# Second feed-forward re-ordered so that down pieces alternate with block pieces; rope scores with 128 rows

## The chip, the core and the metric

The kernel runs on one core of one Trainium2 chip. Its time is the device time of the whole program in microseconds (us), the median of three runs: 2722.33 us before the change (2721.0 to 2722.39). Five engines work side by side and meet at semaphores: TensorE (PE, matmuls; its weight loads are shown apart as PEld), VectorE (DVE), ScalarE (ACT), GpSimd (POOL) and SyncE (SP, which here starts all weight transfers).

## The reference

Two transformer blocks run one after the other on 256 tokens of width 2048, in float32. Cut to what the change touches:

```python
# first block: attention with 16 heads; a head has 128 plain and 64 rotated (rope) dimensions
q = concat([q[..., :128], apply_rope(q[..., 128:], positions)])
k = concat([k[..., :128], apply_rope(k[..., 128:], positions)])
s = einsum('bqhd,bkhd->bhqk', q, k) * scale        # causal softmax, then times v
x = x + (silu(h2 @ w_ffn_gate) * (h2 @ w_ffn_up)) @ w_ffn_down     # width 5632
# second block: stick-breaking attention, spatial gating, then
h2 = rms_norm(x, g_ff)
x = x + square(relu(h2 @ w_ff1)) @ w_ff2            # w_ff1 2048 x 8192, w_ff2 8192 x 2048
```

## The kernel before

Every weight matrix is cut into **pieces** of two 128-row tiles by 512 columns (512 KB). SP brings a piece into a raw buffer (tile R, or tile G for block pieces). ACT rounds it to a shorter float (line 230, "high part", into tile W), DVE subtracts that from the raw numbers (line 232, "low part"), and PE multiplies. A product of two floats is made of three matmuls: high by high, high by low, low by high. The activations stand transposed and split the same way in A, B or C.

There are two kinds of piece. A **plain** piece (`chunk`, lines 262 to 264) is 2 row tiles x 2 token tiles x 3 = 12 matmuls with 512 columns. A **block** piece (`strassen`, lines 315 to 317) treats the same product as a 2 x 2 block product with seven products in place of eight: 7 x 3 = 21 matmuls with 256 columns. It needs three more DVE operations ahead (`sums`, lines 207 to 209, which make the sums of weight blocks) and longer casts (1792 in place of 1024 columns), and at the end of its chunk `fin` (lines 328 to 332) adds the seven products up from PSUM banks 0 to 3. A chunk is the 8 pieces that make 512 output columns of a 2048-row matrix.

All work is a list `jobs`, which `drive` (line 161) emits in order. Before the matmuls of piece k it emits the split (DMA, sums, cast, low part) of the pieces up to k + 3, where a slot of W is free: plain pieces of the feed-forwards rotate over three slots, block pieces over two. Each engine executes its own instructions strictly in the order of emission and waits at semaphores. `run` entries of the list (transposes, evictions) stand between pieces.

In the first feed-forward `braid` mixes a plain chunk (gate) with a block chunk (up) in the order p p s p s p s p s p s p s p s s, where p is plain and s is block. In the second, groups of two such braids (an ff1 chunk that is plain, the next that is block) are followed by the down product `w_ff2` in plain pieces: 4 chunks of 8 pieces for each of the four groups. So 8 of its 16 ff1 chunks are block chunks. A down chunk collects in banks (4, 5), (0, 1), (4, 5), (2, 3) and is added to the residual X on DVE (`ev_acc`, line 907, or `ev_out`, line 1206, which also writes the output). `t_a` transposes 512 columns of activations into B (8 PE transposes, 2 casts, 2 low parts). At the start of each feed-forward `transposed_s` makes the last quarter of its input with sums of blocks (lines 361 to 379).

In the attention `s_pair` makes the scores of two heads, eight groups of three matmuls: four for the 128 plain dimensions, and four for the 64 rope dimensions, whose operands lie on partitions 0 to 63 for one head and 64 to 127 for the other (`hp`).

Of the kernel before, what the change touches and what calls it, by code (L numbers as in the profile page):

```python
# [15 lines left out]
P = 128  # L16
# [8 lines left out]
RAWS = 3  # L25
QW = 256
PLAIN, MIX, STR = 0, 1, 2
AHEAD = {PLAIN: 4, MIX: 3, STR: 3}
# [43 lines left out]
def body(tc, d, out):  # L72
# [4 lines left out]
    with tc.manual_schedule(), \  # L77
# [80 lines left out]
        SLOTS = {PLAIN: range(6), MIX: range(3), STR: range(6, 8)}  # L158

        def drive():  # L160
# [3 lines left out]
            seen_h, seen_r, cnt = {}, {}, {}  # L164
            for i, j in enumerate(pcs):
                kind = j[5]

                def cells(s):
                    a, b, w = hslots(s)
                    return [(o + x) // 256 for o in (a, b) for x in range(0, w, 256)]  # L170

                last, s = min((max(seen_h.get(x, -1) for x in cells(s)), s) for s in SLOTS[kind])
                num.append(s)
                free_h.append(last)
                seen_h.update((x, i) for x in cells(s))
                rk = kind == STR
                m = cnt.get(("r", rk), 0)
                cnt[("r", rk)] = m + 1
                slot = (rk, m % (RAWS if rk else RAW))
                rnum.append(slot[1])  # L180
                free_r.append(seen_r.get(slot, -1))
                seen_r[slot] = i
            raws, hl, used = {}, {}, [-1]
            nd, nt, ns = [0], [0], [0]

            def dma():
                while nd[0] < len(pcs) and free_r[nd[0]] < ns[0] and nd[0] < ns[0] + 2 * RAW:
                    i = nd[0]
                    if i in before_dma:
                        before_dma[i]()  # L190
                    src = pcs[i][1]
                    a, n = src.shape[1], src.shape[2]
                    if pcs[i][5] == STR:
                        t = G[:, 2048 + 2048 * rnum[i] : 4096 + 2048 * rnum[i]]
                    else:
                        t = R[:, 1024 * rnum[i] : 1024 * rnum[i] + 1024]
                    sync.dma_start(t[:, : a * n].rearrange("p (a b) -> p a b", a=a), src)
                    raws[i] = t
                    nd[0] += 1

            def sums(upto):

                while nt[0] <= min(upto, nd[0] - 1):
                    i = nt[0]
                    if pcs[i][5] == STR:
                        v = raws[i].rearrange("p (a b) -> p a b", a=8)
                        dve.tensor_tensor(v[:, 4:6, :], v[:, 0:4:3, :], v[:, 1::-1, :], op=ALU.subtract)  # L207
                        dve.tensor_tensor(v[:, 6, :], v[:, 3, :], v[:, 4, :], op=ALU.subtract)  # L208
                        dve.tensor_tensor(v[:, 7, :], v[:, 2, :], v[:, 6, :], op=ALU.subtract)
                    nt[0] += 1  # L210

            def split(upto):
                while ns[0] <= min(upto, len(pcs) - 1) and free_h[ns[0]] <= used[0]:
# [9 lines left out]
                    if kind == STR:  # L223
                        n, a = 1792, 7
                        t = t[:, 256:]
# [16 lines left out]
            for j in jobs:  # L242
                if j[0] == "run":
                    j[1]()
                else:
                    split(k + AHEAD[j[5]])
                    assert ns[0] > k
                    j[2](*hl.pop(k))
                    used[0] = k
                    k += 1  # L250

# [44 lines left out]
        def strassen(pair, forms, w, kts, c0, evict, later=False):  # L296
# [3 lines left out]
            prod = [(("x", 0, 0), 0, 2, 1), (("x", 1, 0), 1, 0, 0), (("s", 3), 2, 3, 0), (("x", 1, 1), 6, 2, 0),  # L300
                    (("s", 0), 3, 1, 1), (("s", 1), 5, 0, 1), (("s", 2), 4, 1, 0)]

            def mk(j):
                def fn(h, l):
                    opened = set()
                    for x, wi, bank, half in prod:
                        o = PS[:, bank * 512 + half * QW : bank * 512 + (half + 1) * QW]
                        if x[0] == "x":
                            xh, xl = pair(2 * j + x[1], x[2])
                        else:  # L310
                            xh, xl = forms[:, 0, j, x[1], :], forms[:, 1, j, x[1], :]
                        first = j == 0 and bank not in opened
                        opened.add(bank)
                        last = j == kts // 2 - 1
                        pe.matmul(o, xh, h[:, wi, :], start=first, stop=False, skip_group_check=True)  # L315
                        pe.matmul(o, xl, h[:, wi, :], start=False, stop=False, skip_group_check=True)  # L316
                        pe.matmul(o, xh, l[:, wi, :], start=False, stop=last, skip_group_check=True)  # L317
                return fn

            for j in range(kts // 2):  # L320
                items.append(piece(wsrc(w, 2 * j, c0, 512), mk(j), kind=STR))

            def fin():
                q = PS[:, 0:2048].rearrange("p (a b) -> p a b", a=8)
                u = rview(G, 1024, 4, QW)
# [3 lines left out]
                dve.tensor_tensor(u[:, 0:2, :], v[:, 0:1, :].to_broadcast(bc), q[:, 0:2, :], op=ALU.add)  # L329
                dve.tensor_tensor(u[:, 2:4, :], u[:, 1:2, :].to_broadcast(bc), q[:, 2:4, :], op=ALU.add)  # L330
                dve.tensor_tensor(v[:, ::-1, :], u[:, 2:3, :].to_broadcast(bc), q[:, 3:5, :], op=ALU.add)
                dve.tensor_tensor(u[:, 3, :], u[:, 3, :], q[:, 6, :], op=ALU.add)
# [3 lines left out]
            def ends():  # L336
                evict(0, rview(G, 1024, 4, QW)[:, 0:4:3, :])
# [5 lines left out]
        def braid(a, b, inject=None):  # L343

            pa, pb = [x for x in a if x[0] == "pc"], [x for x in b if x[0] == "pc"]
            order = [pa[0], pa[1]]
            for i in range(6):
                order += [pb[i], pa[i + 2]]
            order += [a[-1], pb[6], pb[7], b[-1]]
            for at in sorted(inject or {}, reverse=True):  # L350
                order.insert(at, ("run", inject[at]))
            return order

        def transposed_s(nat, pair, forms, kts, gain):

            x4, s4 = rview(G, 0, 2, 2, NT, P), rview(G, 1024, 2, 4, P)
# [14 lines left out]
            split2(pair.v[:, 0, kts[0] : kts[0] + 4, :], pair.v[:, 1, kts[0] : kts[0] + 4, :], rview(G, 0, 4, S))  # L371
# [304 lines left out]
        qkT = rview(B, 4096, 2, 6, S)  # L676
        pT = [rview(B, 4096 + 3072, 2, 512), rview(C, 2048, 2, 512)]
# [5 lines left out]
        def zero_pT():  # L683
            for t in pT:
                pool.memset(t[:, :, 0:P].bitcast(F32), 0.0)

# [34 lines left out]
        def t_pair(p):  # L721
# [12 lines left out]
            split2(qkT[:, 0, 4:6, :], qkT[:, 1, 4:6, :], bank.rearrange("p (a b) -> p a b", a=2))  # L734

        def s_pair(p):
            rq = rqs[p % 2]
            banks = []
            for h in range(2):
                bank = aux_tile()  # L740
                banks.append(bank)
                for qt in range(NT):
# [3 lines left out]
                    hp = slice(64 * h, 64 * h + 64)  # L746
                    mm3(o, [qkT[hp, i, 4, qs] for i in range(2)], [qkT[hp, i, 5, :] for i in range(2)], False, True)
# [143 lines left out]
        abuf = rview(G, 0, NT, 512)  # L891
# [22 lines left out]
        for gi, (c0, nch) in enumerate(groups):  # L914
            aT = pairat(B, 0, 16)
            for j in range(nch):
                c = c0 + j
                jobs.extend(braid(chunk(h2T, "w_ffn_gate", KT, c * 512, 512, ev_silu, kind=MIX, fixed=(4, 5)),
# [279 lines left out]
        def half(tok, i):  # L1198

            v = rview(G, 1024, 4, QW)[:, 0:4:3, :] if tok == 0 else tmp.rearrange("p (a b) -> p a b", a=2)  # L1200
# [10 lines left out]
        pending = {4: pending}  # L1211
        for gi in range(4):
            aT = pairat(B, 0, 16)
            for j in range(0, 4, 2):
                c = 4 * gi + j
                plain = chunk(h2T, "w_ff1_2", KT, c * 512, 512, lambda tok, ps: relu2(abuf[:, tok, :], tok, ps),
                              kind=MIX, fixed=(4, 5))
                block, ends = strassen(h2T, h2F, "w_ff1_2", KT, (c + 1) * 512, lambda tok, v: relu2(v, tok, v), later=True)
                jobs.extend(braid(plain, block, pending))
                pending = {1: t_a(aT, blocks(abuf), j), 2: ends, 7: t_a(aT, half, j + 1)}  # L1220
            for oc in range(4):
                inj = None
                if oc == 0:
                    inj = {1: pending[2], 2: pending[1], 4: pending[7]}
                    pending = None
                ev = ev_out(oc) if gi == 3 else ev_acc(oc)
                jobs.extend(chunk(aT, "w_ff2_2", 16, oc * 512, 512, ev, row0=16 * gi, inject=inj,
                                  kind=MIX, fixed=DOWN[oc]))


# [17 lines left out]
def blockwise(name, c):  # L1248

    return name == "w_ffn_up" or (name == "w_ff1_2" and c % 2 == 1)  # L1250
# [62 lines left out]
```

## Time and profile before

| | |
|---|---|
| median of three runs | 2722.33 us |
| the profiled execution's own time | 2722.61 us |
| its span, first to last instruction | 2720.9 us |
| PE busy | 2709.6 us (100%) |
| PEld busy | 2278.4 us (84%) |
| DVE busy | 1851.8 us (68%) |
| ACT busy | 1402.6 us (52%) |
| DMA | 506.66 MB, mean 186 GB/s |

The busy time of an engine is the part of the span in which at least one of its instructions was under way. Matmuls are pipelined, so that one that begins every 234 ns may show 400 ns. How fast PE really goes is read from the distances between the starts of its matmuls. The span is 1.7 us shorter than the execution's time.

### The profile page before, as it was taken

The page shows a single profiled execution, that of the slowest core. Times are in us where ns is not written, and L with a number is a line of the kernel's source. Part 1 is how long each engine was busy: PE and PEld are TensorE (multiplying, and loading weights), DVE is VectorE, ACT ScalarE, POOL GpSimd, SP SyncE. Part 2 cuts the span into 40 slices and gives each one's busy share as a digit, 9 for nine tenths or more (in the row PEclk, how much of TensorE's full clock was granted, in tenths as well). Part 3 has the DMA queues.
Part 4 walks back from the last instruction along what each step waited for, and adds up shares of the span by engine and source line. Part 5 has one row for each costly group of instructions (what it writes and reads, how often), then busy time and mean ns, then how long its engine had stood idle before and what let it go on. Part 6 is the DMA issues. An engine that isn't in the chain of part 4 may idle for free. (4 is left out here: it accounts for less than half of the span.)

```text
span 2720.9 us, 35965 instructions
## 1 busy us (share of the span) xinstructions
PE 2709.6 (100%) x13996; PEld 2278.4 (84%) x13996; DVE 1851.8 (68%) x2233; ACT 1402.6 (52%) x1749; POOL 73.0 (3%) x153
## 2 busy tenths in 40 slices
PE   9999999999999999999999999999999999999999
PEld 8988888888888888888888888888888888898887
DVE  6555667766996699579755565455678486685774
ACT  6544666545654455345455555544556355464553
POOL 1000111000000000000000010000000000000000
PEclk9999999999999999999999999999999999999999
DMA  7666534554555555565555554555555555655555
GB/s 255 212 212 201 168 127 146 177 180 172 200 187 179 202 206 186 180 210 185 177 196 172 192 183 166 188 188 181 173 180 182 190 200 177 208 179 185 209 176 164
DMA packets 143179, 506.66 MB, mean 186 GB/s; under 512 B 16160, under 2 KB 18592, under 8 KB 142496
## 3 DMA queue, kind: packets, MB, share of 16 engines
q1 hardware_dynamic: 142864, 504.31, 54.8%
q8 instruction: 109, 1.79, 0.3%
q14 instruction: 62, 0.51, 0.1%
q10 hardware_dynamic: 144, 0.05, 0.0%
HBM read 502.21 MB, written 2.10 MB: 185 GB/s over the span
## 5 line engine op out<-in xcount | busy, mean ns | idle before, releaser
L232 DVE TENSOR_TENSOR W<-R,W 128x1024 fp32r<-128x1024 f32 (+2 forms) x795 | 943.5, 1208 | 508.8 <-ACT W L230 505.4
L230 ACT CAST W<-R 128x1024 fp32r<-128x1024 f32 (+2 forms) x798 | 810.7, 1035 | 532.1 <-PE PS L264 445.1
L263 PE MATMUL PS<-W,A 128*128 128x512 f32 (+2 forms) x1728 | 677.8, 392 | 3.2 <-DVE W L232 3.1
L262 PE MATMUL PS<-W,A 128*128 128x512 f32 (+2 forms) x1728 | 678.5, 393 | 0.6 <-ACT W L230 0.4
L264 PE MATMUL PS<-W,A 128*128 128x512 f32 (+2 forms) x1728 | 675.8, 391 | 0.0
L262 PE MATMUL PS<-W,B 128*128 128x512 f32 (+1 forms) x1248 | 492.0, 394 | 0.0
L263 PE MATMUL PS<-W,B 128*128 128x512 f32 (+1 forms) x1248 | 489.4, 392 | 0.9 <-DVE W L232 0.9
L264 PE MATMUL PS<-W,B 128*128 128x512 f32 (+1 forms) x1248 | 489.3, 392 | 0.0
L230 ACT CAST W<-G 128x1792 fp32r<-128x1792 f32 x152 | 257.5, 1694 | 304.7 <-PE PS L316 173.6
L264 PEld LDWEIGHTS PS<-W,A 128*128 128x128 f32 x1728 | 323.9, 187 | 73.7
L263 PEld LDWEIGHTS PS<-W,A 128*128 128x128 f32 x1728 | 324.4, 188 | 72.5 <-DVE W L232 6.6
L262 PEld LDWEIGHTS PS<-W,A 128*128 128x128 f32 x1728 | 324.2, 188 | 68.3 <-ACT W L230 0.8
L232 DVE TENSOR_TENSOR W<-G,W 128x1792 fp32r<-128x1792 f32 x152 | 307.0, 2020 | 40.6 <-ACT W L230 40.6
L263 PEld LDWEIGHTS PS<-W,B 128*128 128x128 f32 x1248 | 234.1, 188 | 54.6 <-DVE W L232 1.8
L264 PEld LDWEIGHTS PS<-W,B 128*128 128x128 f32 x1248 | 233.9, 187 | 54.2
L262 PEld LDWEIGHTS PS<-W,B 128*128 128x128 f32 x1248 | 234.0, 188 | 53.7
L317 PE MATMUL PS<-W,C 128*128 128x256 f32 x608 | 169.8, 279 | 0.0
L315 PE MATMUL PS<-W,C 128*128 128x256 f32 x608 | 169.8, 279 | 0.0
L316 PE MATMUL PS<-W,C 128*128 128x256 f32 x608 | 169.4, 279 | 0.0
L315 PE MATMUL PS<-W,A 128*128 128x256 f32 x456 | 128.6, 282 | 0.0
L317 PE MATMUL PS<-W,A 128*128 128x256 f32 x456 | 127.3, 279 | 0.8 <-DVE W L232 0.8
L316 PE MATMUL PS<-W,A 128*128 128x256 f32 x456 | 127.3, 279 | 0.0
(231 smaller groups left out, 2481.5 us busy)
## 6 DMA issues: line engine op xcount, KB each, us to landing
R<-in_w_in_dram SPq DMA_DIRECT2D x224, 512.0 KB, 4.5
R<-in_w_ff_dram SPq DMA_DIRECT2D x192, 512.0 KB, 3.6
R<-in_w_ffn_gate_dram SPq DMA_DIRECT2D x88, 512.0 KB, 4.4
G<-in_w_ffn_up_dram SPq DMA_DIRECT2D x88, 512.0 KB, 3.5
R<-in_w_ffn_down_dram SPq DMA_DIRECT2D x88, 512.0 KB, 3.5
R<-in_w_out_dram SPq DMA_DIRECT2D x64, 512.0 KB, 4.3
G<-in_w_ff_dram SPq DMA_DIRECT2D x64, 512.0 KB, 3.5
R<-in_w_attn_o_dram SPq DMA_DIRECT2D x32, 512.0 KB, 4.2
```

What stands on the lines that cost most here:

```text
L230: act.copy(hv, v)
L232: dve.tensor_tensor(lv, v, hv.bitcast(F32), op=ALU.subtract)
L262: pe.matmul(o, x[0], w[0], start=first, stop=False)
L263: pe.matmul(o, x[0], w[1], start=False, stop=False)
L264: pe.matmul(o, x[1], w[0], start=False, stop=last)
L315: pe.matmul(o, xh, h[:, wi, :], start=first, stop=False, skip_group_check=True)
L316: pe.matmul(o, xl, h[:, wi, :], start=False, stop=False, skip_group_check=True)
L317: pe.matmul(o, xh, l[:, wi, :], start=False, stop=last, skip_group_check=True)
```

## The change

There are three parts.

1. **Second feed-forward.** All ff1 chunks from number 2 on are block chunks (14 of 16, `blockwise`), and their pieces alternate with the pieces of the down product of earlier chunks: p s p s ... over 16 pieces (`merge`, `HALF`). In the chunks 3 to 15 the fifth piece is computed in the plain way, but into the same seven-product banks (`flat_fn`, 24 matmuls with 256 columns, kind MIX). The down product is taken in 8 groups of 4 pieces per output chunk (before: 4 groups of 8), so twice as many `ev_acc` are made, and they all collect in banks (4, 5) until the tail. Chunk 0 stands alone as a plain chunk; the gate and up pieces of the first feed-forward go through `merge` too, in the order p s p s.
2. **Block pieces.** The seven products are sorted by bank (0, 1, 2, 3; in the last piece of a chunk 2, 0, 1, 3). The last sum of weight blocks overwrites the first raw block, so a raw buffer is 1792 columns in place of 2048, and chunks from 4 on use four of them (STR4). `mate` stays empty, so `sums` works on one piece at a time as before.
3. **Rope scores.** The keys' rope part of each head gets a slot of its own with 128 rows, of which the other head's 64 are zero (set once by POOL), so that the rope matmuls use all 128 rows. The split of rope queries and keys is 3 casts and 3 low parts in place of one of each. The buffer `pT[0]` moves from B to C.

```diff
-        def braid(a, b, inject=None):
-            pa, pb = [x for x in a if x[0] == "pc"], [x for x in b if x[0] == "pc"]
-            order = [pa[0], pa[1]]
-            for i in range(6):
-                order += [pb[i], pa[i + 2]]
-            order += [a[-1], pb[6], pb[7], b[-1]]
...
+        def merge(pattern, a, b, inject=None):
+            lists, order, n = {"p": list(a), "s": list(b)}, [], 0
+            for c in pattern:
+                if inject and n in inject:
+                    order.append(("run", inject[n]))
+                src = lists[c]
+                order.append(src.pop(0))
+                n += 1
+                while src and src[0][0] == "run":
+                    order.append(src.pop(0))
...
+        BRAID, HALF = "psp" + "sp" * 6 + "s", "ps" * 8
...
+                if kind == STR4:
+                    r = 4 + len(blocks_at) % 4
+                    blocks_at.append(i)
+                else:
+                    r = min((seen_r.get(x, -1), x) for x in (range(5, 8) if kind == STR else range(RAW)))[1]
...
-                        dve.tensor_tensor(v[:, 7, :], v[:, 2, :], v[:, 6, :], op=ALU.subtract)
+                        dve.tensor_tensor(v[:, :, 0, :], v[:, :, 2, :], v[:, :, 6, :], op=ALU.subtract)
...
+                    order = (2, 0, 1, 3) if j == kts // 2 - 1 else (0, 1, 2, 3)
+                    for x, wi, bank, half in sorted(prod, key=lambda t: order.index(t[2])):
...
+                def flat_fn(h, l):
+                    h, l = (t.rearrange("p a (b c) -> p (a b) c", b=2) for t in (h, l))
+                    for kt, tok, wi, bank, half in flat:
+                        three(at(bank, half), pair(2 * j + kt, tok), h[:, wi, :], l[:, wi, :], False, ...)
+                return flat_fn if j in plain else fn
...
-                dve.tensor_tensor(u[:, 3, :], u[:, 3, :], q[:, 6, :], op=ALU.add)
+                if plain:
+                    ends_at = (U[:, 3:4, :], v[:, 1:2, :])
+                    for o, x in zip(ends_at, (q[:, 6:7, :], q[:, 7:8, :])):
+                        dve.tensor_tensor(o, o, x, op=ALU.add)
...
-            split2(qkT[:, 0, 4:6, :], qkT[:, 1, 4:6, :], bank.rearrange("p (a b) -> p a b", a=2))
+            split2(qkT[:, 0, 4, :], qkT[:, 1, 4, :], bank[:, 0:S])
+            for h in range(2):
+                hp = slice(64 * h, 64 * h + 64)
+                split2(qkT[hp, 0, 5 + h, :], qkT[hp, 1, 5 + h, :], bank[hp, S:])
...
-                    hp = slice(64 * h, 64 * h + 64)
-                    mm3(o, [qkT[hp, i, 4, qs] for i in range(2)], [qkT[hp, i, 5, :] for i in range(2)], False, True)
+                    mm3(o, [qkT[:, i, 4, qs] for i in range(2)], [qkT[:, i, 5 + h, :] for i in range(2)], False, True)
...
+        jobs.extend(at_pieces(ff1(0), {3: pending}))
+        block, ends = ff1_blocks(2)
+        jobs.extend(merge(BRAID, ff1(1), block, {3: t_c(0, blocks(abuf))}))
+        pending = {1: t_c(1, blocks(abuf)), 2: ends, 7: t_c(2, half)}
+        for c in range(3, 16):
+            g, o = (c - 3) // 2, 2 * ((c - 3) % 2)
+            block, ends = ff1_blocks(c, (4,), STR4 if c > 3 else STR)
+            jobs.extend(merge(HALF, down(g, o, (4, 5)) + down(g, o + 1, (4, 5)), block, pending))
+            pending = {2: ends, 7: t_c(c, half)}
+        tail = down(6, 2, (4, 5)) + down(6, 3, (0, 1))
+        for oc in range(4):
+            tail += down(7, oc, [(2, 3), (4, 5), (0, 1), (2, 3)][oc])
+        jobs.extend(at_pieces(tail, {2: ends, 5: t_c(15, half)}))
```

How the order of instructions moves is shown for DVE at two places. The first is the start of the first feed-forward, from the end of the last `transposed_s` on. Before:

```order
L379 TENSOR_TENSOR A<-G,A 128x1024
L379 TENSOR_TENSOR C<-G,C 128x1024
L232 TENSOR_TENSOR W<-R,W 128x1024
L207 TENSOR_TENSOR G<-G 128x512
L208 TENSOR_TENSOR G<-G 128x256
L209 TENSOR_TENSOR G<-G 128x256
L232 TENSOR_TENSOR W<-G,W 128x1792
```

And now (line 242 is the old 232, 218 to 220 are the old 207 to 209, 417 is the old 379):

```order
L417 TENSOR_TENSOR A<-G,A 128x1024
L417 TENSOR_TENSOR C<-G,C 128x1024
L218 TENSOR_TENSOR G<-G 128x512
L219 TENSOR_TENSOR G<-G 128x256
L220 TENSOR_TENSOR G<-G 128x256
L242 TENSOR_TENSOR W<-G,W 128x1792
```

The piece that PE needs next after the transposes' cover is used up, the eighth of the braid, was a plain one and is a block one now, and the sums of the block piece after it stand ahead of its low part.

The second place is the end of an ff1 block chunk in the second feed-forward. Before, a braid of two ff1 chunks (line 329 is the first addition of `fin`):

```order
L207 TENSOR_TENSOR G<-G 128x512
L208 TENSOR_TENSOR G<-G 128x256
L209 TENSOR_TENSOR G<-G 128x256
L232 TENSOR_TENSOR W<-G,W 128x1792
L329 TENSOR_TENSOR G<-tmp,PS 128x512
L330 TENSOR_TENSOR G<-G,PS 128x512
L331 TENSOR_TENSOR tmp<-G,PS 128x2x256
L332 TENSOR_TENSOR G<-G,PS 128x256
L232 TENSOR_TENSOR W<-R,W 128x1024
```

And now, a chunk from number 4 on (line 951 is `ev_acc`, the old 907; 354 to 360 are `fin`):

```order
L242 TENSOR_TENSOR W<-G,W 128x1792
L951 TENSOR_TENSOR X<-X,PS 128x512 x2
L242 TENSOR_TENSOR W<-R,W 128x1024
L354 TENSOR_TENSOR G<-tmp,PS 128x512
L355 TENSOR_TENSOR G<-G,PS 128x512
L356 TENSOR_TENSOR tmp<-G,PS 128x2x256
L360 TENSOR_TENSOR G<-G,PS 128x256
L360 TENSOR_TENSOR tmp<-tmp,PS 128x256
L218 TENSOR_TENSOR G<-G 128x512
L219 TENSOR_TENSOR G<-G 128x256
L220 TENSOR_TENSOR G<-G 128x256
L242 TENSOR_TENSOR W<-G,W 128x1792
```

The two evictions of a down chunk stand behind the low part of the next chunk's first block piece, and `fin` has one addition more, 256 columns for the eighth PSUM half that only the plain piece of the chunk uses.

## Rows read from the trace of the kernel before

**Rows 1.** The page, busy us (share of the span) and instructions of each engine.

```profile
PE 2709.6 (100%) x13996; PEld 2278.4 (84%) x13996; DVE 1851.8 (68%) x2233; ACT 1402.6 (52%) x1749; POOL 73.0 (3%) x153
```

**Rows 2.** Waits of PE over the span: total us, times, longest us.

```profile
PE PS L263 <- DVE W L232: 4.1, 6, 0.9
```

**Rows 3.** Timeline of PE: start us, us, engine, line; a plain, then a block piece.

```profile
684.33 0.40 PE L262 MATMUL PS<-W,A 128*128 128x512 f32 x1
...
685.73 0.39 PE L262 MATMUL PS<-W,A 128*128 128x512 f32 x1
...
687.79 0.28 PE L315 MATMUL PS<-W,C 128*128 128x256 f32 x1
...
688.84 0.28 PE L315 MATMUL PS<-W,C 128*128 128x256 f32 x1
```

**Rows 4.** Timeline of PE, the scores of one pair of heads.

```profile
338.62 0.28 PE L262 MATMUL PS<-B 128*128 128x256 f32 x1
...
339.07 0.39 PE L262 MATMUL PS<-B 64*128 64x256 f32 x1
...
342.90 0.50 PE L262 MATMUL PS<-W,B 128*128 128x512 f32 x1
...
343.70 0.40 PE L262 MATMUL PS<-W,B 128*128 128x512 f32 x1
```

**Rows 5.** Groups of PE, 290 to 620 us: count | busy us, mean ns | idle.

```profile
L262 PE MATMUL PS<-B 64*128 64x256 f32 x32 | 12.2, 383 | 0.0
```

**Rows 6.** Groups of DVE by form, 1995 to 2720 us (the second feed-forward).

```profile
L232 DVE TENSOR_TENSOR W<-R,W 128x1024 fp32r<-128x1024 f32 x194 | 236.5, 1223 | 169.8 <-ACT W L230 169.1
L232 DVE TENSOR_TENSOR W<-G,W 128x1792 fp32r<-128x1792 f32 x64 | 129.3, 2020 | 21.3 <-ACT W L230 21.3
L207 DVE TENSOR_TENSOR G<-G 128x512 f32<-128x512 f32 x64 | 43.8, 684 | 2.0 <-DMA G<-in_w_ff_dram 2.0
...
L208 DVE TENSOR_TENSOR G<-G 128x256 f32<-128x256 f32 x64 | 27.2, 425 | 2.2
...
L907 DVE TENSOR_TENSOR X<-X,PS 128x512 f32<-128x512 f32 x24 | 15.3, 681 | 0.0
...
L332 DVE TENSOR_TENSOR G<-G,PS 128x256 f32<-128x256 f32 x8 | 3.3, 414 | 0.0
```

**Rows 7.** Groups of ACT by form, 756.44 to 799.65 us (one braid, first feed-forward).

```profile
L230 ACT CAST W<-G 128x1792 fp32r<-128x1792 f32 x8 | 13.5, 1693 | 19.6 <-DVE G L209 9.9 <-PE PS L316 8.1 <-PE PS L317 1.6
```

**Rows 8.** The same braid: us, busy of PE, PEld, DVE, ACT, POOL, PEclk, DMA, GB/s.

```profile
756.44:799.65 43.21, 43.21 (x274) 38.36 (x272) 41.20 (x49) 23.61 (x21) 0.00 (x0) 1.00 0.56 196
```

**Rows 9.** Timeline of DVE at the braid's beginning: the evictions of the chunk before.

```profile
754.41 0.68 DVE L329 TENSOR_TENSOR G<-tmp,PS 128x512 f32<-128x512 f32 x1
...
757.64 0.74 DVE L899 SCALAR_TENSOR_TENSOR G<-tmp,st,G 128x512 f32<-128x512 f32 x1
```

**Rows 10.** Timeline of PE at the same place.

```profile
756.43 0.39 PE L264 MATMUL PS<-W,A 128*128 128x512 f32 x1
756.75 0.36 PE L315 MATMUL PS<-W,A 128*128 128x256 f32 x1
```

**Rows 11.** Timeline of DVE, start of the first feed-forward, from the low part shown above.

```profile
682.49 1.22 DVE L232 TENSOR_TENSOR W<-R,W 128x1024 fp32r<-128x1024 f32 x1
683.62 0.69 DVE L207 TENSOR_TENSOR G<-G 128x512 f32<-128x512 f32 x1
```

**Rows 12.** Timeline of PE at the same place; in brackets the wait.

```profile
682.70 0.39 PE L262 MATMUL PS<-W,A 128*128 128x512 f32 x1
683.76 0.50 PE L263 MATMUL PS<-W,A 128*128 128x512 f32 x1 [0.68 <-DVE W L232]
...
687.22 0.39 PE L317 MATMUL PS<-W,A 128*128 128x256 f32 x1 [0.39 <-DVE W L232]
```

**Rows 13.** Timeline of PE, start of the second feed-forward.

```profile
2025.66 0.50 PE L263 MATMUL PS<-W,A 128*128 128x512 f32 x1 [0.92 <-DVE W L232]
...
2029.12 0.39 PE L317 MATMUL PS<-W,A 128*128 128x256 f32 x1 [0.40 <-DVE W L232]
```

More of the change, by code (lines that the diff above doesn't have):

```diff
@@ L305, in fn @@
                     opened = set()
[L306 to L312, printed above, removed]
-                        opened.add(bank)
[L314 to L318, printed above, removed]
+                    order = (2, 0, 1, 3) if j == kts // 2 - 1 else (0, 1, 2, 3)
+                    for x, wi, bank, half in sorted(prod, key=lambda t: order.index(t[2])):
+                        xs = pair(2 * j + x[1], x[2]) if x[0] == "x" else [forms[:, i, j, x[1], :] for i in range(2)]
+                        three(at(bank, half), xs, h[:, wi, :], l[:, wi, :], j == 0 and bank not in opened,
+                              j == kts // 2 - 1)
+                        opened.add(bank)
+                def flat_fn(h, l):
+                    h, l = (t.rearrange("p a (b c) -> p (a b) c", b=2) for t in (h, l))
+                    for kt, tok, wi, bank, half in flat:
+                        three(at(bank, half), pair(2 * j + kt, tok), h[:, wi, :], l[:, wi, :], False,
+                              (bank, half) == (3, 1) and kt == 1 and j == max(plain))
+                return flat_fn if j in plain else fn
+            assert 0 not in plain and kts // 2 - 1 not in plain
             for j in range(kts // 2):
-                items.append(piece(wsrc(w, 2 * j, c0, 512), mk(j), kind=STR))
+                items.append(piece(wsrc(w, 2 * j, c0, 512), mk(j), kind=MIX if j in plain else kind))
             def fin():
                 q = PS[:, 0:2048].rearrange("p (a b) -> p a b", a=8)
-                u = rview(G, 1024, 4, QW)
                 v = tmp.rearrange("p (a b) -> p a b", a=2)
@@ L1210, in body @@
         stage(MIX)
[L1211 to L1228, printed above, removed]
+        aT = pairat(B, 0, 16)
@@ new lines, in ff1, with ff1_blocks, down @@
+        def ff1(c):
+            return chunk(h2T, "w_ff1_2", KT, c * 512, 512, lambda tok, ps: relu2(abuf[:, tok, :], tok, ps),
+                         kind=MIX, fixed=(4, 5))
+        def ff1_blocks(c, plain=(), kind=STR):
+            return strassen(h2T, h2F, "w_ff1_2", KT, c * 512, lambda tok, v: relu2(v, tok, v), later=True, plain=plain, kind=kind)
+        def down(g, oc, fixed):
+            at = 8 * (g % 2)
+            return chunk(Pair(aT.v[:, :, at : at + 8, :]), "w_ff2_2", 8, oc * 512, 512, (ev_out if g == 7 else ev_acc)(oc),
+                         row0=8 * g, kind=MIX, fixed=fixed)
```

97 lines of the change are left out of this document (59 added, 38 removed).

## The prediction

> **What bounds the kernel.** I read the page first: PE is busy for 2709.6 of 2720.9 us [rows 1]. Then the waits of PE: the largest entry of the whole program is 4.1 us in six waits for DVE's low part [rows 2]. So PE works without a break, and only two things change the time: the length of its own work, and new waits. Busy time can't give the length, since matmuls overlap in the records; the distance of starts can. In the timeline the reader is to see six plain matmuls begin in 685.73 - 684.33 = 1.40 us, 0.234 us each, and nine block matmuls in 688.84 - 687.79 = 1.05 us, 0.117 us each [rows 3]. A plain piece is then 12 x 0.234 = 2.81 us and a block piece 21 x 0.117 = 2.46 us. The third view is the stretch of one braid: in 43.21 us DVE is busy for 41.20, the granted clock is 1.00 (2.4 GHz), and DMA moves 196 GB/s at a share of 0.56 [rows 8]. DVE is therefore the engine that new waits would come from. ACT with 23.61 us is not.
>
> **Block pieces in the second feed-forward.** Before, 8 chunks x 8 = 64 pieces are block pieces; after, 8 of chunk 2 and 7 of each of the chunks 3 to 15, 8 + 13 x 7 = 99. Thirty-five plain pieces become block pieces, and each saves 12 x 0.234 - 21 x 0.117 = 0.351 us: -12.3 us. The fifth piece of the chunks 3 to 15 is 24 matmuls x 0.117 = 2.81 us, as much as a plain piece. The down product keeps its 128 pieces, and the transposes their number. All of this lies on PE, which sets the end, so it counts in full as long as the pieces are ready in time.
>
> **Are they ready?** A chunk from 4 on has the 16 pieces of the braid of rows 8, with one block piece made plain. On DVE that takes away a low part of 2.02 and the sums 0.684 + 2 x 0.425, in all 3.55 us, and two operations of line 899 (0.74 each [rows 9]), 1.48; it adds a plain low part, 1.22, one addition in `fin`, 0.41, and four evictions of 0.68, 2.72 [rows 6]. 41.20 - 3.55 - 1.48 + 1.22 + 0.41 + 2.72 = 40.5 us. PE takes 43.21 + 0.35 = 43.6 us. DVE's share falls from 95% to 93%, so it has about 3 us in each chunk to make up for a delay.
>
> The tight place is a chunk's end, since each of its two down products collects in banks 4 and 5, and the next one's first matmul must wait until the two evictions have read them. Let the last block piece run from -2.46 to 0. The last down piece ended at -2.46, and the one before began it at -5.27, when the W slot of the next block piece comes free. ACT casts it until about -3.5 (1.69 [rows 7]), DVE's low part follows until -1.5 and stands ahead of the evictions, which end at -0.85 and -0.2. PE wants bank 4 at 0 and bank 5 at 0.70: 0.85 us to spare. Then come a plain low part (to 1.0) and `fin`, five operations of 0.68 and 0.41, to 1.7, 2.3, 2.9, 3.3 and 3.7. The next block piece begins at 2.81, with bank 0 (read by 1.7), then bank 1 at 3.51 (2.9), bank 2 at 4.2 and bank 3 at 4.9 (3.7). The new order of banks has the block piece write first what `fin` reads first. In the middle of a chunk a block piece and eight transposes, over 3 us, cover the evictions. I charge 0.1 us for each of 13 chunk ends, +1.3, for restarts. Bounds: 0, and 13 x 0.7 = 9 if DVE comes 1.55 us later than this.
>
> The Trainium skill (VectorE: DVE Perf Modes, Terms) says that DVE flushes its pipeline after every operation and that the next can't issue until it is empty. The trace shows a low part of 1.22 us begun at 682.49 and the next operation at 683.62, 1.13 us later [rows 11]: they overlap by some 0.1 us. If durations simply added, DVE's share would come closer to PE's time (a rival, below).
>
> **Rope scores.** One pair of heads makes 24 matmuls with 256 columns. They take 342.90 - 338.62 = 4.28 us [rows 4], against 24 x 0.117 = 2.81 by rows 3. The 64-row groups are where PE loses time: there are 32 of these groups [rows 5], and around each the engine leaves the 128-row form and returns to it. The plain matmuls behind the last one need 0.80 us for the first three instead of 0.70 [rows 4], 0.10 more. With 128 rows throughout, the whole excess goes: 8 pairs x (4.28 - 2.81 + 0.10) = -12.6 us. Nothing waits there: no wait on B stands among PE's. The split grows from one cast and one low part of 512 columns to three of 256: about 3 x 0.42 - 0.68 = +0.6 us on DVE and as much on ACT, beside the 4.2 us of two q pieces (24 x 0.175, an estimate at three quarters of rows 3 for 384 columns). I take it as hidden; without that cover it costs 8 x 0.6 = 5 us. The two POOL memsets come once, behind work long done.
>
> **Start of the second feed-forward.** The two waits of 0.92 and 0.40 us [rows 13] come from DVE, which has the last `transposed_s` and the first block pieces to do at once. Now chunk 0 is plain, and the block pieces begin eight pieces later. Each such wait costs about 0.15 us more than its bracket (683.76 - 682.70 - 0.234 = 0.83 for 0.68 [rows 12]): -1.6 us. I bound it at 0 (the waits come back at the first block piece) and -1.8 (both go with all their restarts).
>
> **Start of the first feed-forward.** Its waits of 0.68 and 0.39 us cost 1.4 us with their restarts. In the new order the eighth piece is a block piece. DVE is free for it at 682.49 [rows 11], makes the next sums first (0.684 + 2 x 0.425 = 1.53, to 684.0) and its low part (2.02, to 686.0). PE comes to it at 682.70 as before (a block piece fewer behind the transposes, one more ahead) and wants the low part with its third matmul, at 682.93: 3.1 us of wait in place of 1.4, +1.7. Bounds 0 and +2.5.
>
> **Chunk ends of the first feed-forward.** A braid of 43.21 us has 8 x 2.81 + 8 x 2.46 = 42.1 us of pieces; the remaining 1.1 us is eight transposes and small waits such as the one at 756.75, where the start comes 0.32 us after the last [rows 10] because `fin`, at 754.41 [rows 9], stands behind two block pieces in a row. These are apart now, but the next block piece comes one plain piece sooner. I take -1.0 us over eleven braids; bounds -2.4 and +3.3 (0.3 us more at each).
>
> **Sum.** -12.3 + 1.3 - 12.6 - 1.6 + 1.7 - 1.0 = -24.5 us. From the profiled 2722.6 us this is 2698.1; that execution stands 0.3 us above the median, so 2697.8 us.
>
> **Rivals.**
> *DVE comes late in every chunk.* For it: 93% with waits in between, and 0.85 us of slack. Against: the braids with 95% run with almost no wait. With 0.3 to 0.9 us more at each of 13 ends: 2702 to 2710.
> *The bank pair (4, 5) decides, slower.* The evictions stand behind a low part that DVE only begins when its backlog is done. If DVE ends each chunk a whole block piece (3.55 us) behind, PE waits 3.55 - 0.85 = 2.7 at each end, 35 us in all: 2733. It is slower than before from a backlog of 2.8 us on. The rule of the skill above leads here: added up, 7 x 3.55 + 9 x 1.22 + 2.86 for `fin` + 2.72 + 1.37 for the transposes' low parts is 42.8 of 43.6 us, and a backlog would never be made up. Rows 8 and 11 speak against it: the braid's operations would add up to 8 x 3.55 + 8 x 1.22 + 2.45 + 1.48 + 1.37 = 43.5 us, and are busy for 41.20.
> *The rope groups gain nothing.* If what separates them were a wait and not the change of form, 2710. For it: nothing is seen to release them; against: all groups have the same excess.
> The Trainium skill (TensorE: Matmul & The Clock Gate, Part 3: Packing small matmuls) says that matmuls on different halves of the rows run side by side, so that 128 zero-padded rows would give up a pairing. Rows 4 show no pairing: the eight groups need more time than 24 matmuls one behind the other. By that rule 48 of the 96 rope matmuls are added, 48 x 0.117 = 5.6 us, in place of the gain: 2716.
> *All goes better.* No waits at all: 2692 and below.
>
> **Chances.** Forecast (2693 to 2702) 0.65; DVE late 0.15; bank pair, slower 0.03; rope without gain 0.06, with the lost pairing 0.01; better 0.10. What a measurement can tell from no change is 0.2%, 5.4 us. Only the slower rival and a part of the late one end beyond 2717: faster 0.95, same 0.02, slower 0.03. The range 2691.5 to 2706 leaves out the rope rivals, the slower one and half of the late one.
>
> **What would show it.** In the second feed-forward PE's plain and block starts stay 0.234 and 0.117 apart, a chunk takes 43.6 us, and DVE is busy for about 40 us of it. Waits of line 274 (the old 262) for line 951 would show the bank pair; waits of 276 or of the third block matmul for the low part, a late DVE. The scores of a pair take 2.8 us. In the first feed-forward one wait of some 3 us stands where there were two. If the second feed-forward's chunks take over 45.5 us, the prediction is wrong.

## The result and the profile after

The changed kernel takes 2704.0 us (median; 2702.8 to 2704.7) against 2722.2 us: ratio 0.9934, 95% interval 0.9916 to 0.9951. The profiled span went from 2720.9 to 2702.8 us. The forecast was 2697.8 us in a range of 2691.5 to 2706: the sign and the range hold, and the time is 6.2 us later than forecast. The experiments find 6 to 7 us in the rope part; the misses of the other terms nearly cancel. In number the result lies where the forecast had priced a rival, DVE late in every chunk (2702 to 2710), and that did not happen.

The page of the changed kernel, answering to [rows 1]: PE still works through the whole span, in 471 more and shorter matmuls, and DVE does 116 us more.

```profile
PE 2687.9 (99%) x14467; PEld 2291.7 (85%) x14467; DVE 1968.2 (73%) x2423; ACT 1430.8 (53%) x1771; POOL 74.5 (3%) x155
```

The waits of PE in the changed kernel (total us, times, longest us), answering to [rows 2]. The second, fourth and seventh are new: the transposes of the probabilities waiting for the softmax, a down piece waiting for an eviction, and rope scores waiting for their split.

```profile
PE PS L275 <- DVE W L242: 2.6, 5, 0.8
PE PS L816 <- DVE X L810: 2.1, 2, 1.9
PE PS L324 <- DVE W L242: 1.4, 2, 1.2
PE PS L274 <- DVE X L951: 1.2, 1, 1.2
...
PE PS L274 <- ACT B L416: 0.5, 2, 0.2
```

To see what all this is worth I took, for each matmul of PE, the distance to the next start less the one that its form keeps when nothing disturbs it (0.234 us for 512 columns, 0.175 for 384, 0.117 for 256), and summed this excess by stretch. The cells are good to about 0.4 us. Columns three to five are runs of the experiments below.

| excess, us | before | changed | casts first | raw order | no plain |
|---|---|---|---|---|---|
| up to 300 us | 2.9 | 2.8 | 2.9 | 3.2 | 2.7 |
| attention | 14.3 | 8.6 | 2.2 | 2.2 | 2.2 |
| start of 1st FF, and the 30 us before | 2.5 | 2.5 | 3.0 | 2.6 | 3.3 |
| rest of 1st FF | 3.7 | 2.2 | 2.2 | 2.2 | 2.1 |
| between | 2.4 | 2.4 | 2.4 | 2.4 | 2.4 |
| start of 2nd FF | 1.9 | 1.8 | 1.8 | 1.8 | 1.8 |
| its first chunks | 0.3 | 2.0 | 2.0 | 0.3 | 1.1 |
| its rest | 1.1 | 1.1 | 1.1 | 1.1 | 1.1 |
| sum | 28.9 | 23.2 | 17.4 | 15.5 | 16.6 |

From before to changed the excess falls by 5.7 us. The spans differ by 18.1; the other 12.4 us are the 35 shorter pieces (35 x 0.351 = 12.3).

Two chunks of the second feed-forward (windows; columns as in [rows 8]): PE has no gap, DVE is busy for 40.55 us, as worked out (40.5). A chunk takes 43.22, not 43.6 us.

```profile
2147.10:2190.30 43.20, 43.20 (x277) 38.78 (x276) 40.55 (x49) 24.43 (x24) 0.00 (x0) 1.00 0.55 195
2190.32:2233.54 43.22, 43.22 (x277) 38.80 (x276) 40.55 (x49) 24.43 (x24) 0.00 (x0) 1.00 0.57 196
```

The scores of a pair, timeline of PE, answering to [rows 4]: from the first of 24 matmuls to the plain matmul behind them 2.87 us, and that one's successor comes after 0.24.

```profile
337.27 0.28 PE L274 MATMUL PS<-B 128*128 128x256 f32 x1
...
340.14 0.40 PE L274 MATMUL PS<-W,B 128*128 128x512 f32 x1
340.38 0.40 PE L275 MATMUL PS<-W,B 128*128 128x512 f32 x1
```

So the change of form costs nothing any more, in the pairs where the operands are ready: six of the eight take 2.86 or 2.87 us. The last two take 3.76 and 4.23 us. The scores of the last pair, timeline of PE (in brackets the idle time before):

```profile
495.52 0.28 PE L274 MATMUL PS<-B 128*128 128x256 f32 x1
496.09 0.39 PE L275 MATMUL PS<-B 128*128 128x256 f32 x1 [0.29 <-DVE B L420]
...
496.81 0.38 PE L274 MATMUL PS<-B 128*128 128x256 f32 x1 [0.23 <-ACT B L416]
```

First ScalarE, then VectorE, at the last pair's split:

```profile
496.39 0.37 ACT L416 CAST B<-PS 64x256 fp32r<-64x256 f32 x1 [2.76 <-DVE B L417]
497.24 0.37 ACT L416 CAST B<-PS 64x256 fp32r<-64x256 f32 x1 [0.48 <-DVE B L417]
497.64 1.05 ACT L240 CAST W<-R 128x1024 fp32r<-128x1024 f32 x1
```

```profile
492.89 1.22 DVE L242 TENSOR_TENSOR W<-R,W 128x1024 fp32r<-128x1024 f32 x1
494.03 0.68 DVE L417 TENSOR_TENSOR A<-PS,A 128x512 fp32r<-128x512 f32 x1
494.63 1.40 DVE L420 SCALAR_TENSOR_TENSOR B<-PS,cols,B 128x512 fp32r<-128x512 f32 x2
495.95 0.41 DVE L417 TENSOR_TENSOR B<-PS,B 128x256 fp32r<-128x256 f32 x1
496.79 0.42 DVE L417 TENSOR_TENSOR B<-PS,B 64x256 fp32r<-64x256 f32 x1 [0.43 <-ACT B L416]
```

Of the three casts of this split the two on 64 rows wait: each begins when VectorE has made the low part of the part before it, and VectorE has four other operations to do ahead of the first of these low parts. ScalarE's in-order queue stands for 2.76 and 0.48 us, with the next weight cast behind it. The trace shows that the casts wait, not why: they don't read what the low part writes, but all three parts lie in one PSUM bank, which both engines read. The softmax is late in consequence, and PE stands before the last transposes:

```profile
505.12 0.39 PE L276 MATMUL PS<-W,A 128*128 128x512 f32 x1
507.40 1.00 PE L816 MATMUL PS<-cst,X 128*128 128x128 f32 x6 [1.89 <-DVE X L810]
...
509.09 0.63 PE L274 MATMUL PS<-W,A 128*128 128x512 f32 x1
509.52 0.63 PE L275 MATMUL PS<-W,A 128*128 128x512 f32 x1
```

The last two rows are 0.43 us apart instead of 0.234; more on that at the end. Of what attention loses here, about 2.2 us are in the scores of the last two pairs, 2.4 in front of the transposes of the probabilities and 1.5 in the slower matmuls behind them.

### The profile page after: what moved, and what is told of

Read it like the earlier page. It is cut to its first block, busy times and chain, and to the rows that moved or that the text cites. A ratio compares the mean times of both kernels' runs of the same rounds, so it can differ in the third digit from the quotient of the medians.

```text
span 2702.8 us, 37068 instructions
## 1 busy us (share of the span) xinstructions
PE 2687.9 (99%) x14467; PEld 2291.7 (85%) x14467; DVE 1968.2 (73%) x2423; ACT 1430.8 (53%) x1771; POOL 74.5 (3%) x155
## 4 chain that ended last, share of the span: by engine, by line
PE 72%; DVE 2%; issue 0%; ACT 0%; DMA 0%; DVEq 0%; ACTq 0%
PE PS L275 18%; PE PS L276 18%; PE PS L274 18%; PE PS L324 6%; PE PS L322 6%; PE PS L323 6%; PE PS L429 1%; DVE W L242 1%; DVE G L218 0%; DMA G<-in_w_ff_dram 0%; DVE G L219 0%; DVE A L417 0%; ACT G L401 0%; PE PS L399 0%; ACT W L240 0%
## 5 line engine op out<-in xcount | busy, mean ns | idle before, releaser
L242 DVE TENSOR_TENSOR W<-R,W 128x1024 fp32r<-128x1024 f32 (+2 forms) x760 | 901.8, 1206 | 392.8 <-ACT W L240 387.9
L240 ACT CAST W<-R 128x1024 fp32r<-128x1024 f32 (+2 forms) x763 | 774.1, 1034 | 414.4 <-PE PS L276 296.2
L274 PE MATMUL PS<-W,A 128*128 128x512 f32 (+2 forms) x1536 | 604.1, 393 | 1.2 <-ACT W L240 0.6
L275 PE MATMUL PS<-W,A 128*128 128x512 f32 (+2 forms) x1536 | 601.5, 392 | 1.7 <-DVE W L242 1.7
L276 PE MATMUL PS<-W,A 128*128 128x512 f32 (+2 forms) x1536 | 600.6, 391 | 0.0
L240 ACT CAST W<-G 128x1792 fp32r<-128x1792 f32 x187 | 316.5, 1692 | 313.4 <-PE PS L323 200.3
L242 DVE TENSOR_TENSOR W<-G,W 128x1792 fp32r<-128x1792 f32 x187 | 377.8, 2020 | 33.8 <-ACT W L240 33.5
L276 PEld LDWEIGHTS PS<-W,A 128*128 128x128 f32 x1536 | 288.2, 188 | 65.5
L274 PEld LDWEIGHTS PS<-W,A 128*128 128x128 f32 x1536 | 288.6, 188 | 62.7 <-ACT G L1239 1.3
L275 PEld LDWEIGHTS PS<-W,A 128*128 128x128 f32 x1536 | 288.8, 188 | 61.7 <-DVE W L242 3.0
L322 PE MATMUL PS<-W,C 128*128 128x256 f32 x748 | 208.8, 279 | 0.4 <-DVE tmp L356 0.4
L324 PE MATMUL PS<-W,C 128*128 128x256 f32 x748 | 208.6, 279 | 0.0
L323 PE MATMUL PS<-W,C 128*128 128x256 f32 x748 | 208.6, 279 | 0.0
L324 PE MATMUL PS<-W,A 128*128 128x256 f32 x665 | 185.9, 280 | 1.4 <-DVE W L242 1.4
L322 PE MATMUL PS<-W,A 128*128 128x256 f32 x665 | 187.1, 281 | 0.0
L323 PE MATMUL PS<-W,A 128*128 128x256 f32 x665 | 185.3, 279 | 0.0
```

What stands on the lines that cost most here:

```text
L240: act.copy(hv, v)
L242: dve.tensor_tensor(lv, v, hv.bitcast(F32), op=ALU.subtract)
L274: pe.matmul(o, x[0], w[0], start=first, stop=False)
L275: pe.matmul(o, x[0], w[1], start=False, stop=False)
L276: pe.matmul(o, x[1], w[0], start=False, stop=last)
L322: pe.matmul(o, x[0], h, start=first, stop=False, skip_group_check=True)
```

## Experiments

**Rope part alone and taken away.** The edit, added to the kernel before (e1), or undone in the changed one (e2):

```diff
-            split2(qkT[:, 0, 4:6, :], qkT[:, 1, 4:6, :], bank.rearrange("p (a b) -> p a b", a=2))
+            split2(qkT[:, 0, 4, :], qkT[:, 1, 4, :], bank[:, 0:S])
+            for h in range(2):
+                hp = slice(64 * h, 64 * h + 64)
+                split2(qkT[hp, 0, 5 + h, :], qkT[hp, 1, 5 + h, :], bank[hp, S:])
...
-                    mm3(o, [qkT[hp, i, 4, qs] for i in range(2)], [qkT[hp, i, 5, :] for i in range(2)], False, True)
+                    mm3(o, [qkT[:, i, 4, qs] for i in range(2)], [qkT[:, i, 5 + h, :] for i in range(2)], False, True)
```

> The kernel before with the rope part of the change alone. The prediction's price of this part was 12.6 us (2709.8 us). The traces of before and after, compared stretch by stretch over attention, give 5.7 us. Theory A (the split in three parts hands the work to and fro between ScalarE and VectorE and so makes the last pairs late, which eats the other 7 us) and theory B (the softmax of the last pairs is late whatever the split's order, since the scores are shorter) both expect about 2716.5 us here. If the loss belongs to something else of the changed kernel, this run comes out near 2709.8 us.

> The changed kernel with the rope scores back on 64 rows, everything else of the change kept. If the parts add up, and rope is worth what the traces say, 2704.0 + 5.7 = 2709.7 us; if rope is worth the 12.6 us of the prediction and something else gave 7 us back, 2716.6 us. Every matmul between 64 and 128 rows should show its 0.1 us again in attention, and the 1.9 us wait of the last pair's transposes (line 816 of the changed kernel) should be gone.

Measured: 2715.9 us, 6.4 less than its 2722.3 (ratio 0.9977, 0.9967 to 0.9986), and 2710.6 us, 6.6 more than the changed kernel. Both sides agree: the rope part as written gives 6.5 us, half of the 12.6 forecast, and loses the rest within itself. The wait of the last transposes is in e1 (waits of PE; line 778 is the old 772) and not in e2:

```profile
PE PS L778 <- DVE X L772: 2.1, 2, 1.9
```

**The split in another order.**

```diff
-            split2(qkT[:, 0, 4, :], qkT[:, 1, 4, :], bank[:, 0:S])
-            for h in range(2):
-                hp = slice(64 * h, 64 * h + 64)
-                split2(qkT[hp, 0, 5 + h, :], qkT[hp, 1, 5 + h, :], bank[hp, S:])
+            for hp, i, src in parts:
+                act.copy(qkT[hp, 0, i, :], src)
+            for hp, i, src in parts:
+                dve.tensor_tensor(qkT[hp, 1, i, :], src, qkT[hp, 0, i, :].bitcast(F32), op=ALU.subtract)
```

> The changed kernel, with only the split of the rope bank written in another order: the three casts on ScalarE one behind the other, then the three subtractions on VectorE. Theory A: the two casts on 64 rows no longer wait 0.4 to 0.5 us each for VectorE (the wait of line 416 for line 417), so the last weight cast behind them starts about 1 us sooner, and with it the evictions and the softmax of the last pair: the 1.9 us wait of the last transposes falls by 1 us or more, the waits of 0.3 to 0.4 us in the pairs ahead go, and with them some of the 1.35 us that the matmuls behind it took at half the clock: 2699 to 2701 us. Theory B: the order of the split does not matter, 2703.5 to 2704.5 us, with the last wait unchanged.

Measured: 2697.1 us (2696.5 to 2698.7; ratio 0.9907, 0.9892 to 0.9922), 6.9 less than the changed kernel: theory A, with more than it asked for. ScalarE's timeline now has the three casts in one row without a wait, and the softmax of the last pair begins at 499.63 instead of 504.32 (1.5 us of that ScalarE had gained before this pair's casts). First a row of the changed kernel, then three of this run:

```profile
504.32 0.49 ACT L803 ACTIVATE X<-X,st 128x128 f32<-128x128 f32 x1 [5.63 <-DVE st L798]
```

```profile
491.75 1.02 ACT L779 CAST B<-PS 128x256 fp32r<-128x256 f32 x3
492.79 1.05 ACT L240 CAST W<-R 128x1024 fp32r<-128x1024 f32 x1
499.63 0.49 ACT L805 ACTIVATE X<-X,st 128x128 f32<-128x128 f32 x1 [5.79 <-DVE st L800]
```

Attention's excess falls to 2.2 us, 12.1 below the 14.3 of before: the rope scores are worth 12.1 us, against 12.6 forecast. Theory B is out.

**Old order in the first feed-forward**, in the changed kernel (e4) and in the fastest one (e9):

```diff
-                jobs.extend(merge(BRAID, chunk(h2T, "w_ffn_gate", ...
+                jobs.extend(braid_old(chunk(h2T, "w_ffn_gate", ...
```

> The changed kernel with the gate and up pieces of the first feed-forward in the old order. The traces say that the new order is worth 1.5 us at the chunks' ends and about nothing at its start: 2705.5 us. The prediction priced the start at 1.7 us to its harm and the ends at 1.0 us to its good, so by it this kernel would be 0.7 us faster: 2703.3 us. The single wait of 1.3 us near 678 us should be gone, and the waits at every chunk's end back.

> The fastest kernel so far (no plain piece, 2692.4 us) with the first feed-forward's pieces in the old order. The same undoing in the changed kernel gave +0.4 us, in a run whose trace lacks the 1.6 us that the changed kernel's own trace lost behind the last pair's late transposes. Here no such wait is near. If the new order is worth the 1.5 us that the traces show at the chunks' ends: 2693.9 us. If it is worth nothing in the end: 2692.4 us.

Measured: 2704.4, and 2694.8 us against 2692.4. In the trace the rest of the first feed-forward has 3.7 and 3.8 us of excess, against 2.2 and 2.1: the new order gives about 1.6 us. The times say less clearly so: e9 is 2.4 us slower, e4 only 0.4, within the spread of its runs (2703.4 to 2705.7). In the profiled executions of e4 and the changed kernel the gain is masked, since e4's attention has 1.6 us less excess (7.0 against 8.6, the half clock told below); that this holds for the other executions too is not shown.

**Buffers by longest unused.**

```diff
-                if kind == STR4:
-                    r = 4 + len(blocks_at) % 4
-                    blocks_at.append(i)
-                else:
-                    r = min((seen_r.get(x, -1), x) for x in (range(5, 8) if kind == STR else range(RAW)))[1]
+                raw = range(4, 8) if kind == STR4 else range(5, 8) if kind == STR else range(RAW)
+                r = min((seen_r.get(x, -1), x) for x in raw)[1]
```

> The kernel with the three casts first (2697.1 us), and the raw buffers of the block pieces given out by longest unused through all of the second feed-forward. In the changed kernel the fourth buffer comes in with chunk 4 and the count begins anew there: piece 733 (the last of chunk 3) uses buffer 5, 735 buffer 4, 737 buffer 5 again; now 737 uses 6. Theory A (the 1.7 us at the end of chunk 3 come from that repeat: SyncE's queue stands 13.2 us for the buffer, the block's data lands late, VectorE idles 2.56 us and the evictions behind its low part come late): 2695.4 us, the wait of 13.2 us on SyncE gone, and the wait of line 274 for line 953 too. Theory B (VectorE is behind because chunk 3 has two chunks' transposes and splits to do): 2697.1 us, the wait stays.

Measured: 2696.3 us (2695.2 to 2696.9), 0.8 us less than the run with the casts first; the profiled span is 1.9 us shorter, 1.7 of it in these chunks. The mechanism is seen. In the changed kernel SyncE's queue over the end of chunk 3 (waits) and VectorE's timeline:

```profile
SPq L199 <- DVE W L242: 38.0, 8, 13.2
```

```profile
2106.99 0.69 DVE L218 TENSOR_TENSOR G<-G 128x512 f32<-128x512 f32 x1 [2.55 <-DMA G<-in_w_ff_dram]
...
2108.52 2.02 DVE L242 TENSOR_TENSOR W<-G,W 128x1792 fp32r<-128x1792 f32 x1
2110.45 1.28 DVE L951 TENSOR_TENSOR X<-X,PS 128x512 f32<-128x512 f32 x2
```

The same wait of SyncE now:

```profile
SPq L196 <- DVE W L239: 37.1, 13, 7.8
```

No single wait is over 7.8 us, the bank-pair wait of PE is gone, and the excess of these chunks is 0.3 us. VectorE was not behind; it had no data.

**No plain piece.**

```diff
-            block, ends = ff1_blocks(c, (4,), STR4 if c > 3 else STR)
+            block, ends = ff1_blocks(c, (), STR4 if c > 3 else STR)
```

> The kernel of the run before, with no plain piece in the chunks 3 to 15: all eight pieces of a chunk are block pieces. PE saves 13 x 0.351 = 4.6 us. VectorE gains a block low part and sums, 2.02 + 1.53, and loses a plain low part and one addition, 1.22 + 0.41: 1.9 us more in a chunk of 42.9 us, 42.4 us busy by the 40.5 of the profile. Theory A (busy time counts, so there is still half a microsecond to spare): 2690.8 us, chunks of 42.9 us. Theory B (VectorE has no room for a delay, each chunk's end waits 0.3 to 0.9 us): 2695 to 2702 us. Theory C (durations add up: 42.8 + 1.9 = 44.7 us in each chunk, and the engine sets the pace): 13 x 1.5 us more than 43.2 us, 2715 us.

Measured: 2692.4 us (2691.7 to 2693.6; ratio 0.9890, 0.9876 to 0.9903), the fastest kernel here: 11.6 us below the changed one. A chunk takes 42.88 us, 0.34 less (the 0.351 of a block piece). Against 2696.3 it gains 3.9 us and not the 4.6 of thirteen block pieces; the first chunks have 0.8 us more excess. Theory A is the nearest. Theory C, durations added, is out by 23 us. But VectorE's starts now follow one another without a pause; a window of 43 us:

```profile
2146.00:2189.00 43.00, 43.00 (x275) 38.59 (x274) 42.31 (x52) 25.21 (x24) 0.00 (x0) 1.00 0.59 199
```

**How much room VectorE has.** One (e11) or four (e12) sums more in each of twelve chunks of that kernel:

```diff
+                        if pcs[i][5] == STR4 and i // 2 % 8 in (3,):       # e12: (0, 2, 4, 6)
+                            dve.tensor_tensor(v[:, :, 0, :], v[:, :, 2, :], v[:, :, 6, :], op=ALU.subtract)
```

> The fastest kernel so far (2692.4 us) with one operation more on VectorE in each of the chunks 4 to 15: the third sum of one block piece is made twice (0.42 us busy, its next start 0.46 us later). Theory A (the busy time counts: 42.3 + 0.4 = 42.7 of 42.87 us): no change, 2692.4 us. Theory B (the distance from start to start counts, and these fill 42.8 of 42.87 us): VectorE sets the pace, 12 x (0.46 - 0.07) = 4.7 us more, 2697.1 us, with PE waiting for the low part of block pieces.

> The same with four operations more in each of the chunks 4 to 15 (every second block piece makes its third sum twice). Theory A (busy time): 42.3 + 1.7 = 44.0 us, 12 x 1.1 = 13 us more, 2705.7 us. Theory B (starts): 42.8 + 4 x 0.46 = 44.6 us, 12 x 1.77 = 21 us more, 2713.6 us, with chunks of 44.6 us and PE idle in each.

Measured: 2696.7 and 2711.9 us; chunks of 43.22 and 44.60 us. A window of e12:

```profile
2144.00:2188.62 44.62, 43.64 (x274) 38.69 (x273) 43.79 (x55) 25.11 (x24) 0.00 (x0) 1.00 0.57 189
```

The times are those of theory B. Three more sums cost 44.60 - 43.22 = 1.38 us, 0.46 each, and from 43.22 back by 0.46 VectorE alone needs an estimated 42.76: 0.12 us to spare in the 42.88 of the kernel without a plain piece. PE waits elsewhere than theory B said, not for the low part but for the bank pair of the forecast's slower rival (waits of PE in e12; line 273 is a down piece, 952 `ev_acc`), at both down chunks of each of twelve; with the restarts that is some 16 of the 19 us:

```profile
PE PS L273 <- DVE X L952: 11.7, 24, 0.5
```

**Old order of the banks.**

```diff
-                    for x, wi, bank, half in sorted(prod, key=lambda t: order.index(t[2])):
+                    for x, wi, bank, half in prod:
```

> The kernel of the first run of this group, with the seven sums of every block piece written to the banks in the order of before (2, 0, 3, 2, 1, 0, 1), the new places of the sums in memory kept. If the new order matters: the block piece behind a chunk's end comes to bank 3 some 0.7 us after its start, and the last addition that reads bank 3 ends 0.9 us after the start, so PE waits 0.2 to 0.6 us at each of 13 chunk ends and about as much at the 11 ends of the first feed-forward: 3 to 9 us slower, with waits of line 322 for lines 356 to 362. If a plain piece between covers all of it: no difference, 2695.4 us.

Measured: 2704.0 us, 7.7 slower than 2696.3. The block piece comes to a bank before the last additions have read it (waits of PE; line 319 is a block matmul, 353 the third addition of `fin`):

```profile
PE PS L319 <- DVE tmp L353: 4.2, 13, 1.2
```

The excess grows by 1.4 us in the first feed-forward and by 6.3 in the second behind its start. In the second the order of the banks is thus what makes `fin` free: twelve of the thirteen waits are there. In the first only one end, at 700 us, waits for `fin` (1.15 us); the other ten show no wait.

**Three raw buffers**, with the plain piece (e8) and without (e10):

```diff
-            block, ends = ff1_blocks(c, (4,), STR4 if c > 3 else STR)
+            block, ends = ff1_blocks(c, (4,), STR)                # e10: ()
```

> The kernel with the three casts first, with three raw buffers for the block pieces throughout, as in the first feed-forward. If three are enough (the first feed-forward alternates plain and block pieces at the same pace and waits for no block's data), the time is that of the first run of this group, 2695.4 us, since nothing changes its count at chunk 4. If the fourth is what keeps the data ahead of VectorE (a buffer is asked for again after 16 us instead of 21), VectorE waits for data in most chunks and PE behind it: 0.3 to 1.5 us in 12 chunks, 2700 to 2714 us.

> The fastest kernel so far (no plain piece, 2692.4 us), with three raw buffers throughout. Theory A: a fourth buffer buys nothing, since three were enough with a plain piece (2696.7 against 2696.3 us): 2692.4 us, no waits of VectorE for data. Theory B: without the plain piece each buffer is asked for 1/8 sooner and VectorE has no slack left (its starts fill 42.8 of 42.9 us), so data that land late cost their full delay: 2695 to 2705 us.

Measured: 2696.7 and 2693.0 us, the same as with four (2696.3 and 2692.4). The fourth buffer buys nothing in either, and the way it was brought in cost the changed kernel its 1.7 us.

## Why the prediction was near, and which step failed

- **Block pieces, -12.3: right.** The spans less the excess leave 12.4, and each of thirteen more such pieces shortened its chunk by 0.34.
- **Rope scores, -12.6: the step that failed.** The matmuls were sized rightly (12.1). What failed is "I take it as hidden" of the split. I priced its length, 0.6 us on each of two engines, and the uncovered case at 5 us; the length was indeed nothing, since the casts first do the same operations and give the whole 12.1. The loss of 6 to 7 us is a hand-over: two of three casts each wait for a low part in VectorE's queue. The step counted operations and left out what is queued ahead of the one waited for. The cover that it named is missing where the loss is largest: the last pair has no q pieces ahead of its scores, only one piece of 2.8 us. That the scores are shorter than before is not the cause; with the casts first they are as short, and these waits of PE are gone.
- **Chunk ends of the second feed-forward, +1.3:** about that size (+1.7), by luck, for the reason is another. None of the twelve later ends costs anything: the chunk of 43.22 us is the sum of its pieces and transposes, and my 43.6 had carried along the small waits of the braid of [rows 8]. The one that costs is a DMA that came late.
- **Start of the first feed-forward, +1.7: zero.** One wait in place of two, as foreseen, but of 1.2 us and not 3.1, in all as much as before. VectorE came to its sums 2.0 us ahead of PE, where I had put 0.2 from [rows 11, 12]; why is not tested. Timeline of VectorE, then PE:

```profile
675.60 0.69 DVE L218 TENSOR_TENSOR G<-G 128x512 f32<-128x512 f32 x1
...
677.13 2.02 DVE L242 TENSOR_TENSOR W<-G,W 128x1792 fp32r<-128x1792 f32 x1
```

```profile
677.63 0.28 PE L322 MATMUL PS<-W,A 128*128 128x256 f32 x1
677.74 0.28 PE L323 MATMUL PS<-W,A 128*128 128x256 f32 x1
679.20 0.39 PE L324 MATMUL PS<-W,A 128*128 128x256 f32 x1 [1.18 <-DVE W L242]
```

- **Chunk ends of the first feed-forward, -1.0:** -1.5 in the traces of the changed kernel and e4, -1.7 in those without a plain piece.
- **Start of the second feed-forward, -1.6: near zero** (-0.1), the bound I had called "the waits come back". PE's waits there are shorter than those of [rows 13], but there are more of them, small ones of VectorE and ScalarE:

```profile
2013.69 0.50 PE L275 MATMUL PS<-W,A 128*128 128x512 f32 x1 [0.47 <-DVE W L242]
2023.52 0.50 PE L274 MATMUL PS<-W,A 128*128 128x512 f32 x1 [0.29 <-ACT G L1239]
```

- **The sum.** The rope part came out 6.9 us worse than its term. The other terms were off by +0.4, -1.7, -0.5 and +1.5 us, which all but cancel; that is luck.
- **Rivals.** DVE late in every chunk did not happen, though the time lies in its stretch; the margin was real, 2.2 us of pauses in a chunk. "Rope gains nothing" had the right place and the wrong mechanism. The bank pair is where the kernel does wait once VectorE has more work than PE, as e12 shows.

## What to carry to other kernels

When one split becomes several, write all of the first engine's parts ahead of all of the second's; otherwise each part inherits the second engine's queue, and whatever stands behind it on the first is late. Price a hand-over by what is queued ahead of the instruction waited for, not by the length of the instruction. When a ring of buffers grows, give out the one unused for longest: a count begun anew can ask for the one just taken.

## What the runs showed of the hardware

VectorE's capacity is counted from start to start. In the kernel without a plain piece the 50 operations of a chunk are busy for 42.2 us and their durations add up to 44.7, but the engine needs 42.76. An operation that does not use the result of the one before begins about 0.08 us before that one's end (a low part of 1.22 us at 2184.39, the next operation at 2185.52); one that does, about 0.03 us behind it. The Trainium skill (VectorE: DVE Perf Modes, Terms) has each operation issue only on an empty pipeline; if the durations of the records are taken as the time until then, their sum would be the pace, and the chunks of 42.88 us lie 1.8 us below it.

A change between matmuls on 64 and on 128 rows makes two starts late, by about 0.1 us each. A pair had eight such changes, and without them its scores and the matmul behind take 12.1 / 8 = 1.5 us less. In the kernel before (timeline of PE), where 0.117 us is the distance without a change, the matmul at 338.86 is the last on 128 rows, and the group on 64 rows begins at 339.07 [rows 4]:

```profile
338.86 0.28 PE L264 MATMUL PS<-B 128*128 128x256 f32 x1
...
339.29 0.28 PE L263 MATMUL PS<-B 64*128 64x256 f32 x1
339.41 0.28 PE L264 MATMUL PS<-B 64*128 64x256 f32 x1
```

In the changed kernel the granted clock fell to half behind the stop of 1.9 us at 505 us, and seven matmuls came 0.43 us apart, 1.5 us lost in all. The kernel with rope alone stood just as long and kept the full clock. The two stretches (windows, granted clock third from the end), the changed kernel and the one with rope alone:

```profile
508.70:512.10 3.40, 3.40 (x10) 2.62 (x9) 3.40 (x6) 2.51 (x4) 0.00 (x0) 0.51 0.58 173
```

```profile
508.40:511.80 3.40, 3.40 (x16) 2.72 (x15) 3.40 (x6) 2.53 (x4) 0.00 (x0) 1.00 0.60 180
```

The program need not decide it. The changed kernel and the one with the casts first execute the same instructions at the start, and PE's first weight matmuls begin within 0.04 us of each other (at 6.4, 7.6 and 8.0 us). Behind these waits one execution had the full clock (1.00, 2.4 GHz) and the other half of it (0.50, 1.2 GHz); the changed kernel, then the casts first:

```profile
8.30:11.50 3.20, 2.66 (x11) 1.59 (x9) 1.76 (x3) 2.75 (x5) 0.00 (x0) 1.00 1.03 398
```

```profile
8.30:11.50 3.20, 3.20 (x9) 2.55 (x8) 1.32 (x3) 2.14 (x4) 0.00 (x0) 0.50 1.03 399
```

So one kernel may lose such 1.5 us in one execution and not in the next. What decides it was not found.
